# Two-part float32r weights-times-values product in the attention of a streaming encoder

## The chip, the cores and the metric

One core of one Trainium2 chip runs the whole program. The metric is device time in microseconds (us) of one execution; the kernel before takes 3136.52 us, the median of three runs (3129.24 to 3139.74).

## The reference

The reference is a two-layer encoder over 1024 positions of width 1024, all in float32. Each layer normalises, projects to 2948 columns (`w_in`), runs four mixers side by side (A: a recurrent scan, B: differential attention, C: spatial gating, D: forgetting attention, each 256 columns wide in 4 heads of 64), projects back (`w_out`), and applies a gated feed-forward with a 3-tap causal convolution. What the change concerns is the last product of B and D:

```
p1 = softmax(where(mask, s1, -1e30)); p2 = softmax(where(mask, s2, -1e30))      # B
o  = einsum('bhqk,bhkd->bhqd', p1 - lam * p2, v)                                 # [128 queries x keys] x [keys x 64]
pr = softmax(where(mask, s, -1e30)); o = einsum('bhqk,bhkd->bhqd', pr, v)        # D
```

A block of 128 queries sees the keys up to its own end, so a block has 1 to 8 groups of 128 keys.

## The kernel before, in words

The sequence is cut into two halves of 512 positions, `hf` 0 and 1. For each layer and half the program does `win` (the input projection), the mixers, `wout`, and `ffn`. The large products (`product`, `product2`, L497 and L505) take float32 weights from HBM 512 KB at a time (`wload`, L487: DMA to `wr`, ACT casts to the float32r high part, DVE subtracts to get the low part, both into `hr`), and form each 128x512 result in PSUM (`pm`, two banks) from three float32r products per 128 rows (`acc3`, L467): high x high, high x low, low x high. One 8-step product is 24 matmuls.

The mixers of one half run beside the large products of another: `body` (L1423) writes out by hand which generator is advanced when (`beside`, `weave`, `side`), and gives priorities (`PRI`). The Tile context is opened with `schedule_with_timeline_sim=True`: from these priorities and a simulated time line it fixes the order of instructions on every engine when the program is built, and the engines run their lists in that order. The half (0, 0) has its mixers beside the conditioning products `ada` of both layers and beside `win` of half (0, 1); the later ones run beside `wout`, `ffn` and `win`. `wout` of a half starts once the mixers of that half are done.

Attention, per head: `prepare` (L983) transposes the values with TensorE (`pv`), copies them (`v`, L1017) and stores them to DRAM (`vv`, tensors vB and vD: four blocks of 128 keys, two slots, 256 columns; only slot 0 is used). `values` (L1042) loads the 64 columns of one head to `V`, one DMA per half of the keys (L1053). For each of four query blocks `scores` (L1056) makes S in PSUM with float32r products, `softmax` (L1070) makes `p` with ACT, and `weighted` (L1090) does three things: TensorE transposes `p` in groups of 128 keys into a `px` bank (L1097), ACT copies up to 512 columns to SBUF (`ct`, L1106), and a float32 product per 128 keys with `ct` as the stationary operand and 64 columns of `V` moving accumulates into another `px` bank (recorded at L186, tile names px<-V,ct). ACT then scales the 128x64 result into `yB` or `yD`. At the end of every second head `out_y` (L1121) transposes y, copies it (`yst`) and stores it to `yT`, from where `wout` loads it (`yr`, split into `yh` and `yl`).

Tiles of the attention come from pool `p2` (14 pages of 128x512 float32: q, k, V, p, ct, y, yst); `prepare` uses pool `q2` (6 pages); `px` has two PSUM banks, shared by transposes and weighted products.

Of the kernel before, what the change touches and what calls it, by code (L numbers as in the profile page):

```python
# [85 lines left out]
class Kern:  # L86
    def __init__(self, tc, es, a):
# [3 lines left out]
        def pool(n, b, **k):  # L91
            return es.enter_context(tc.tile_pool(name=n, bufs=b, **k))

        PS = bass.MemoryType.PSUM
        for n, b in POOLS.items():
            setattr(self, n, pool(n, b))
# [886 lines left out]
    def prepare(self, l, hf, g, hd, finish):  # L983
# [6 lines left out]
        for t0 in (0, 2):  # L990
            ss = self.small([128, 2, ng], "qss" + g)
            xs = []
            for t in (t0, t0 + 1):
# [14 lines left out]
                for u in range(2):  # L1008
                    nc.tensor.transpose(ps[:, u * 128:u * 128 + 128], pv[:, u, :], self.ident)
                if PVR:  # L1010
                    v = self.sq([128, 2, 256], F32R, name="v")
# [30 lines left out]
    def values(self, l, hf, g, h):  # L1042
        nc = self.nc
        if PVR:
            V = []
# [44 lines left out]
    def weighted(self, p, V, scale, out):  # L1090
# [3 lines left out]
        for pc, n in p:  # L1094
            ps = self.misc()
            for j in range(0, n, 128):
                nc.tensor.transpose(ps[:, j:j + 128], pc[:, j:j + 128], self.ident)  # L1097
            if PVR:
                ch = self.s2([128, 512], F32R, name="ch")
# [9 lines left out]
        last = len(cts) - 1  # L1109
        if not PVR:  # L1110
            for b, ct in enumerate(cts):
# [239 lines left out]
NADA = 12  # L1351
MLP = True
YLP = False
PVR = False
PACE, PSTEP = 2, 2
PACING = (1, 0, 0, 0)
PA = 5000
# [18 lines left out]
P2 = True  # L1376
PRI = [(6000, 4000, 4000), (2000, 4000, 2000), (2000, 6000, 4000), (2000, 4000, 2500)]
WC = 16
POOLS = dict(cst=1, xp=8, wr=2, wp=3, hp=32, ar=4, mp=14, nt=8, nn=3, an=2, a1=9, a2=6, sm=2, p2=14, q2=6)
BANKS = dict(pm=2, pS=2, px=2, pa=1, pn=1)  # L1380


# [187 lines left out]
```

## Time and profile before

| | before |
|---|---|
| median of 3 runs | 3136.52 us |
| lowest, highest | 3129.24, 3139.74 us |
| the profiled execution: its time, its span | 3145.82 us, 3144.0 us |
| mean granted TensorE clock | 0.961 |
| PE, PEld, DVE, ACT, POOL busy | 96%, 78%, 63%, 45%, 12% |

PE is TensorE's matmuls and PEld its weight loads, which overlap them; DVE is VectorE, ACT ScalarE, POOL GpSimd, SP the engine that issues the DMAs. A line number is that of the kernel; L186, L189, L195 and L198 are helpers that record nearly every operation, so the groups there are told apart by the tiles' names. A float32 product appears as two LDWEIGHTS and two MATMUL records, a float32r product as one of each. Records print both types as f32 on PE. [...]

### The profile page before, as it was taken

How to read it: one execution, taken by the hardware profiler on the slowest of the kernel's cores; microseconds unless marked ns; L12 is line 12 of the kernel's file. 1: busy time of each engine (PE TensorE's matmuls, PEld its weight loads, DVE VectorE, ACT ScalarE, POOL GpSimd, SP SyncE). 2: the span in 40 equal slices, each digit the busy share in tenths (PEclk: the TensorE clock that was granted, in tenths of full speed). 3: DMA queues.
4: the chain of work that ended last, by engine and by line, in shares of the span. 5: the costliest groups of instructions: out<-in, count | busy, mean ns of one | idle time of the engine just before them, and what ended most of it. 6: DMA issues, size and time to landing. Idle time of an engine off the chain costs nothing. (4 is left out here: it accounts for less than half of the span.)

```text
span 3144.0 us, 48993 instructions
## 1 busy us (share of the span) xinstructions
PE 3020.1 (96%) x17440; PEld 2443.8 (78%) x17440; DVE 1980.0 (63%) x4681; ACT 1413.5 (45%) x2829; POOL 383.2 (12%) x463
## 2 busy tenths in 40 slices
PE   6999988899999999999999999999999999899999
PEld 5777767777877888777888887777888888778887
DVE  4566554567677685357777566368787675455555
ACT  3444632335454545435455443345454464333333
POOL 1010000111111011010111111020111101011111
PEclk8999977799999999999999999999999999899999
DMA  6467576443333334454343323453433232513332
GB/s 247 140 221 227 188 237 206 142 147 92 92 109 104 116 95 147 136 173 131 102 132 90 113 88 131 142 175 100 122 109 107 90 117 66 192 61 94 112 103 74
DMA packets 302195, 414.12 MB, mean 132 GB/s; under 512 B 75520, under 2 KB 174336, under 8 KB 301952
## 3 DMA queue, kind: packets, MB, share of 16 engines
q1 hardware_dynamic: 301952, 411.00, 41.7%
q8 instruction: 138, 2.26, 0.3%
q14 instruction: 105, 0.86, 0.1%
HBM read 347.66 MB, written 63.21 MB: 131 GB/s over the span
## 5 line engine op out<-in xcount | busy, mean ns | idle before, releaser
L186 PE MATMUL pm<-hh,hr 128*128 128x512 f32 (+1 forms) x4352 | 1420.9, 400 | 10.6 <-ACT hh L198 4.6
L186 PEld LDWEIGHTS pm<-hh,hr 128*128 128x128 f32 (+1 forms) x4352 | 813.4, 189 | 194.9 <-ACT hh L198 8.3
L186 PE MATMUL pm<-hl,hr 128*128 128x512 f32 x2176 | 865.4, 398 | 6.6 <-DVE hl L195 6.6
L493 ACT CAST hr<-wr 128x1024 fp32r<-128x1024 f32 (+2 forms) x496 | 427.5, 863 | 701.5 <-PE pm L186 605.0
L189 DVE TENSOR_TENSOR hr<-wr,hr 128x1024 fp32r<-128x1024 f32 (+2 forms) x496 | 511.5, 1032 | 278.3 <-ACT hr L493 254.1
L186 PEld LDWEIGHTS pm<-hl,hr 128*128 128x128 f32 x2176 | 410.7, 189 | 94.7 <-DVE hl L195 10.1
L186 PE MATMUL pm<-mh,hr 128*128 128x512 f32 x1408 | 464.6, 399 | 2.5 <-DVE y L189 1.0
L186 PEld LDWEIGHTS pm<-mh,hr 128*128 128x128 f32 x1408 | 264.0, 188 | 59.4 <-issue 1.2
L195 DVE SCALAR_TENSOR_TENSOR y<-pm,cst,y 128x511 f32<-128x511 f32 (+1 forms) x352 | 261.6, 744 | 74.1 <-ACT y L198 71.0
L195 DVE SCALAR_TENSOR_TENSOR x<-pm,cst,x 128x512 f32<-128x512 f32 x224 | 167.4, 748 | 180.2 <-PE pm L186 179.4
L186 PE MATMUL pm<-ml,hr 128*128 128x512 f32 x704 | 277.2, 394 | 0.0
L642 POOL TENSOR_TENSOR y<-y,y 128x512 f32<-128x512 f32 x88 | 117.2, 1332 | 1250.0 <-DVE y L189 423.0
L1075 DVE TENSOR_REDUCE cst<-S 128x1 f32<-128x512 f32 (+3 forms) x288 | 154.2, 551 | 97.6 <-PE S L186 96.7
L198 ACT ACTIVATE p<-S,cst 128x512 f32<-128x512 f32 (+3 forms) x288 | 165.5, 581 | 79.1 <-DVE cst L189 65.1
L186 PE MATMUL pm<-yh,hr 128*128 128x512 f32 x512 | 172.7, 413 | 6.6 <-ACT yh L600 6.6
L186 PEld LDWEIGHTS px<-V,ct 128*128 128x128 f32 x1152 | 155.3, 201 | 24.3 <-ACT ct L1106 14.2
L186 PE MATMUL px<-V,ct 128*128 128x64 f32 x1152 | 160.3, 282 | 10.6 <-ACT ct L1106 7.3
L198 ACT ACTIVATE y<-pm,cst 128x512 f32<-128x512 f32 x176 | 136.9, 778 | 67.3 <-PE pm L186 66.8
L186 PEld LDWEIGHTS pm<-ml,hr 128*128 128x128 f32 x704 | 132.7, 189 | 25.2
L647 POOL TENSOR_TENSOR ml<-th,mh 128x512 fp32r<-128x512 f32 x88 | 123.9, 1408 | 219.7 <-ACT mh L646 207.8
L189 DVE TENSOR_TENSOR cst<-cst 128x1 f32<-128x1 f32 (+6 forms) x552 | 97.5, 184 | 54.1 <-ACT p L198 46.0
L1106 ACT COPY ct<-px 128x512 f32<-128x512 f32 (+1 forms) x192 | 88.0, 479 | 95.4 <-PE px L1097 92.1
(230 smaller groups left out, 3578.7 us busy)
## 6 DMA issues: line engine op xcount, KB each, us to landing
wr<-in_up SPq DMA_DIRECT2D x176, 512.0 KB
ar<-in_ada SPq DMA_DIRECT2D x192, 256.0 KB
wr<-in_win SPq DMA_DIRECT2D x92, 512.0 KB
wr<-in_down SPq DMA_DIRECT2D x128, 256.0 KB
wr<-in_wout SPq DMA_DIRECT2D x32, 512.0 KB
ks<-qkB SPq DMA_DIRECT2D x192, 64.0 KB
wr<-in_down SPq DMA_DIRECT2D x64, 192.0 KB
k<-qkD SPq DMA_DIRECT2D x72, 128.0 KB
```

Of the source, the lines that this page charges most:

```text
L186: return self.nc.tensor.matmul(out, lhsT, rhs, start=start, stop=stop, **kw)
L189: self.nc.vector.tensor_tensor(out=out, in0=a, in1=b, op=op)
L195: self.nc.vector.scalar_tensor_tensor(out=out, in0=a, scalar=s, in1=b, op0=op0, op1=op1)
L198: self.nc.scalar.activation(out=out, in_=in_, func=func, **k)
L493: self.nc.scalar.copy(out=h, in_=r)
L642: nc.gpsimd.tensor_tensor(out=ya, in0=ya, in1=yg, op=ALU.mult)
L647: (nc.gpsimd if MLP else nc.vector).tensor_tensor(out=ml, in0=th, in1=mh.bitcast(F32), op=ALU.subtract)
L1075: nc.vector.tensor_reduce(out=nm[:, i:i + 1], in_=S_[:, 0:n], axis=AX.X, op=ALU.max, negate=True)
L1106: nc.scalar.copy(out=ct[:, 0:n], in_=ps[:, 0:n])
```

## The change

The flag `PVR` turns on and pool `p2` gets 18 pages in place of 14.

```
-PVR = False
+PVR = True
-POOLS = dict(cst=1, xp=8, wr=2, wp=3, hp=32, ar=4, mp=14, nt=8, nn=3, an=2, a1=9, a2=6, sm=2, p2=14, q2=6)
+POOLS = dict(cst=1, xp=8, wr=2, wp=3, hp=32, ar=4, mp=14, nt=8, nn=3, an=2, a1=9, a2=6, sm=2, p2=18, q2=6)
```

What the flag selects is in the code already. In `prepare`, the values are split: `v[:, 0]` is the ACT copy rounded to float32r, `v[:, 1]` is a DVE subtraction of it from PSUM (L1014), and one DMA stores both slots. In `values`, each half of the keys is loaded to a page of its own, high and low columns side by side (4 x 2 x 64 columns), by one DMA each as before. In `weighted`, the transposed weights are split as they leave PSUM, and each 128 keys take two products:

```
nc.scalar.copy(out=ch[:, 0:n], in_=ps[:, 0:n])
self.tt(cl[:, 0:n], ps[:, 0:n], ch[:, 0:n].bitcast(F32), ALU.subtract)
...
self.mm(ps[:, 0:128], ch, V[b], b == 0, False)
self.mm(ps[:, 0:64], cl, V[b][:, 0:64], False, b == last)
...
self.act(out, ps[:, 64:128], AF.Copy, scale=scale)
self.stt(out, ps[:, 0:64], scale, out, ALU.mult, ALU.add)
```

So high weights meet high and low values (128 moving columns), low weights meet high values (64 columns), and the two column halves of the result are added when it leaves PSUM.

## Rows read from the trace of the kernel before

**Rows 1.** The page's first part (busy us, share of the span, instructions) and a line of its second (tenths in 40 slices of 78.6 us).
```profile
PE 3020.1 (96%) x17440; PEld 2443.8 (78%) x17440; DVE 1980.0 (63%) x4681; ACT 1413.5 (45%) x2829; POOL 383.2 (12%) x463
PEclk8999977799999999999999999999999999899999
```

**Rows 2.** Busy time of each engine by stretches of 157.2 us: stretch, its length, then PE, PEld, DVE, ACT, POOL, each with its instructions, the granted clock, the DMA share and GB/s.
```profile
471.60:628.80 157.20, 138.85 (x1217) 112.10 (x1210) 79.64 (x245) 53.26 (x137) 13.46 (x17) 0.77 0.56 174
...
1414.80:1572.00 157.20, 154.48 (x852) 125.96 (x850) 120.77 (x309) 77.63 (x168) 20.48 (x19) 0.96 0.39 117
...
2200.80:2358.00 157.20, 155.27 (x875) 127.38 (x874) 121.43 (x276) 78.43 (x166) 25.14 (x21) 0.99 0.39 115
...
2672.40:2829.60 157.20, 140.44 (x648) 116.28 (x647) 81.63 (x153) 60.89 (x104) 17.40 (x12) 0.90 0.39 126
```

**Rows 3.** The time line of PE around three float32 products of weights and values at full clock: start us, us, what, count.
```profile
1502.83 0.78 PE L186 MATMUL px<-V,ct 128*128 128x64 f32 x6
1503.45 0.61 PE L1000 MATMUL px<-cst,pt 128*128 128x128 f32 x4
```

**Rows 4.** The same stretch on PEld, the weight loads.
```profile
1502.72 0.75 PEld L186 LDWEIGHTS px<-V,ct 128*128 128x128 f32 x6
1503.34 0.48 PEld L1000 LDWEIGHTS px<-cst,pt 128*128 128x128 f32 x4
```

**Rows 5.** The time line where three float32r products with 128 moving columns stand together (the scores of one 128-key group and the mask), ahead of large products; PE and PEld.
```profile
1169.74 0.44 PE L186 MATMUL S<-k,q 128*128 128x128 f32 x2
...
1169.96 0.19 PEld L186 LDWEIGHTS S<-hr 128*128 128x128 f32 x1
1170.02 0.27 PE L186 MATMUL S<-hr 128*128 128x128 f32 x1
1170.07 0.19 PEld L186 LDWEIGHTS pm<-mh,hr 128*128 128x128 f32 x1
1170.13 0.45 PE L186 MATMUL pm<-mh,hr 128*128 128x512 f32 x1
```

**Rows 6.** The time line of PE where one float32r product with 128 moving columns stands alone among large ones.
```profile
1110.21 0.22 PE L186 MATMUL S<-k,q 128*128 128x128 f32 x1
1110.27 0.45 PE L186 MATMUL pm<-hh,hr 128*128 128x512 f32 x1
```

**Rows 7.** Groups by shape, weight loads and matmuls: count, busy us, mean ns of one, idle time before.
```profile
L186 PEld LDWEIGHTS px<-V,ct 128*128 128x128 f32 x1152 | 155.3, 201 | 24.3 <-ACT ct L1106 14.2 <-issue 2.2 <-ACT Us L848 0.2
L186 PEld LDWEIGHTS pm<-ml,hr 128*128 128x128 f32 x704 | 132.7, 189 | 25.2
L186 PE MATMUL px<-V,ct 128*128 128x64 f32 x1152 | 160.3, 282 | 10.6 <-ACT ct L1106 7.3 <-DVE cst L189 2.8
```

**Rows 8.** Groups by shape on DVE that stand nearest to the new ones (the subtraction of a rounded copy from PSUM, narrower reads of PSUM, and the weights' low parts).
```profile
L189 DVE TENSOR_TENSOR ql<-px,qh 128x512 fp32r<-128x512 f32 x32 | 21.9, 683 | 10.8 <-ACT qh L1036 10.3 <-issue 0.2
L1075 DVE TENSOR_REDUCE cst<-S 128x1 f32<-128x384 f32 x48 | 25.8, 548 | 6.0 <-PE S L186 5.8
L1075 DVE TENSOR_REDUCE cst<-S 128x1 f32<-128x256 f32 x48 | 20.0, 417 | 9.9 <-PE S L186 9.4
L1075 DVE TENSOR_REDUCE cst<-S 128x1 f32<-128x128 f32 x48 | 13.6, 284 | 16.2 <-PE S L186 16.1
L195 DVE SCALAR_TENSOR_TENSOR U<-px,cst,U 128x128 f32<-128x128 f32 x32 | 9.1, 343 | 1.1 <-PE px L186 1.1
L189 DVE TENSOR_TENSOR D<-D,pa 128x64 f32<-128x64 f32 x16 | 3.5, 219 | 22.0 <-PE pa L186 15.6 <-ACT x L1002 6.3
L189 DVE TENSOR_TENSOR hr<-wr,hr 128x1024 fp32r<-128x1024 f32 x300 | 373.8, 1246 | 261.4 <-ACT hr L493 238.7 <-PE pm L186 5.4 <-ACT yD L198 5.3
```

**Rows 9.** Groups by shape on ACT: the copy of transposed weights, a cast of the same shape to float32r, and one of the two output scalings.
```profile
L1106 ACT COPY ct<-px 128x512 f32<-128x512 f32 x96 | 55.3, 586 | 61.2 <-PE px L1097 59.7 <-POOL acc L430 0.6
L1036 ACT CAST qh<-px 128x512 fp32r<-128x512 f32 x32 | 18.7, 585 | 28.5 <-PE px L1032 25.2 <-issue 2.9
L198 ACT ACTIVATE yD<-px,cst 128x64 f32<-128x64 f32 x64 | 20.0, 313 | 44.7 <-PE px L186 44.0
```

**Rows 10.** The time line between 2702 and 2707 us: the last head of D in half 1 of layer 1, where the granted clock is 0.50; three query blocks follow each other.
```profile
2704.07 2.66 PE L186 MATMUL px<-V,ct 128*128 128x64 f32 x12
2704.32 0.37 ACT L1106 COPY ct<-px 128x256 f32<-128x256 f32 x1 [0.50 <-PE px L1097]
2704.37 1.22 DVE L189 TENSOR_TENSOR hr<-wr,hr 128x1024 fp32r<-128x1024 f32 x1
2706.98 0.31 ACT L198 ACTIVATE yD<-px,cst 128x64 f32<-128x64 f32 x1
```

**Rows 11.** The chain that ended last, in order of time, as it passes from that head to `wout`: start us, us, what.
```profile
2723.72 0.85 PE px L186 x8
...
2724.60 0.32 ACT yD L198
...
2724.97 0.34 PE px L1125
...
2731.66 1.65 PE pm L186 x3
```

**Rows 12.** DMA: the page's line on its main queue (packets, MB, share of 16 engines' span) and the loads of V from vB.
```profile
q1 hardware_dynamic: 301952, 411.00, 41.7%
...
V<-vB SPq DMA_DIRECT2D x24, 128.0 KB
```

## The prediction, made before the change was built

> **What bounds the kernel now.** I read the page's engine shares first: PE is busy 96% of the span, DVE 63%, ACT 45% [rows 1]. The table of stretches then shows that this is no mean over unlike stages: from 1400 us on PE is near 98% wherever large products run, DVE reaches 77% at most, and the granted clock is 0.96 to 1.00. Two kinds of stretch differ: the half-0 mixers of layer 0 beside the conditioning products (clock 0.77, PE 139 of 157 us) and the end of the last mixers (clock 0.90, PE 140 of 157 us) [rows 2]. So PE's list of instructions, one behind the other, sets the end; what lies on another engine costs only where PE comes to an instruction whose input is late. The question for the change is thus threefold: does PE's own list get shorter, do waits get longer where PE has cover, and what happens at the stage ends, where it has none.
>
> **PE's list.** The number of float32 products is 576: a half has 8 heads (B and D), half 0 sees 1+2+3+4 = 10 groups of keys per head, half 1 sees 5+6+7+8 = 26, so 8 x 36 x 2 layers. Each is two weight loads and two matmuls, hence the 1152 of each [rows 7]. The change removes them and adds 576 float32r products with 128 moving columns and 576 with 64, each one load and one matmul: again 1152 and 1152. What does one cost? Six old records start at 1502.83 and the next product starts at 1503.45, 0.62 us for six [rows 3]; their loads start at 1502.72 and end their turn at 1503.34, the same 0.62 us [rows 4]. The first of the six started while its own load was already done, so five or six loads fill the time: 0.10 to 0.12 us each. Now the float32r form: three products with 128 columns start at 1169.74 and the next large one at 1170.13; the last of the three takes 0.11 us to its successor, and its load stands 0.11 us before the next load [rows 5]. A single one among large products lets the next start after 0.06 us, but that next one then takes 0.45 us where its neighbours take 0.40, so 0.11 us is paid in all [rows 6]. The load itself lasts 201 ns (float32) against 189 ns (float32r) [rows 7]. I therefore take 0.11 us a record before and after, set by the 128 columns of stationary operand, which the change does not reduce: 1152 x 0 = **0 us**. Bounds: all records at the bare 0.06 us would give 1152 x (0.06 - 0.11) = -58 us; with 0.12 us against 0.11 it is +12 us.
>
> The row says that the short product is paid by its load. [...]
>
> **DVE.** Added are 192 subtractions `cl` (96 of 512 columns, 32 each of 384, 256 and 128), priced by the same subtraction in the rows, 683 ns, and for narrower ones by reads of PSUM of that width, 548, 417 and 284 ns: 65.6 + 17.5 + 13.3 + 9.1 = 105.5 us. To these come 128 final sums of 128x64 out of PSUM, between 219 and 343 ns, nearer the first by width; at 0.25 us 32 us. And 32 subtractions of values, 417 ns, 13 us [rows 8]. Together 151 us: DVE goes from 1980 to 2131 us, 68%. In its fullest stretches it has 121 of 157 us [rows 2]; some 10 to 13 of the 192 fall in each, with their sums 10 us, so 84%. PE's large products cover this. If the cover went, all 151 us would be the price.
>
> **ACT** keeps its count: the high part takes the place of the copy, 585 against 586 ns, and the scaling of 313 ns stays [rows 9]. 0 us.
>
> **DMA and SP.** No issue is added. Each of 48 loads of V (128 KB) doubles, 6.3 MB and 24,576 packets; at the mean packet (41.7% of 16 engines' 3144 us over 301,952 packets, 69 ns) that is at most 107 us of all sixteen together, at the mean rate per MB 20 us, on engines 42% used [rows 12]. Hidden, as V is asked for ahead of the query block; the cover is thinnest at a last head. Pages: a half-1 head of D holds before q, two, k, four, V, one, y, one, p, two, ct, two: 12 of 14, and the next p the rest; afterwards 15 of 18 with one page spare behind the next p. B in half 1 goes from 14 of 14 to 17 of 18. The four pages replace what V, ch and cl take; I give them nothing.
>
> **Waits that get longer.** V's products need the output bank of `px`; with two banks it comes free only when the first group of transposed weights has left, which now needs ACT's copy and then DVE's `cl`. And the output bank is held through ACT's scaling and then DVE's sum. Per query block the chain grows by 0.28 to 0.68 us plus 0.25 us. Queued behind `cl` on DVE are the softmax maxima of the next block and the low parts of the large products' weights, 1246 ns each [rows 8].
>
> *Stage ends.* Where the last head of D closes a half, blocks follow each other with little else: at 2704 us twelve V products, a copy, a 1.22 us weight subtraction on DVE in between, and the scaling to yD [rows 10]. From the last V products the chain runs through yD and the transposes to `wout` [rows 11]. I count three such ends: this one and, by the code, those of both halves of layer 0, where `wout` waits for the mixers too. Four blocks x (0.68 + 0.25) = 3.7 us for one, 11 us for three; PE still has scores of the next block to do, so I take half, **+6 us**, bounds 0 and +11.
>
> *Elsewhere.* PE stood 7.3 us and 2.8 us before V's products for ACT's copy and a DVE operation, its loads 14.2 us [rows 7]. Now a second wait stands behind the first, on the fuller engine: I add as much again, **+10 us**. Bounds: 0, and 128 blocks x 0.93 us = +119 us if nothing covered it.
>
> **Sum:** 0 + 0 + 6 + 10 = +16 us. The profiled execution took 3145.8 us (span 3144.0), 9.3 us over the median of the three; +16 us on it is 3162 us, and against the median, which I forecast, 3152 us, 0.5% slower.
>
> **Rivals.** *Hidden (no change).* The order is planned by a simulated time line, which sees the new steps too and may place V's products later, behind large ones; PE's waits stay at some 10 us. For: waits are that small now in spite of a similar chain [rows 7]. Against: the stage ends leave little to place. 3137 to 3145 us.
>
> *The load is no limit (faster).* If float32r products of 64 or 128 columns follow each other at 0.06 us, 1152 x 0.05 = 58 us go: 3079 us; without the waits' cover 3095 us. For: the bare start distance [rows 6]. Against: the 0.11 us between loads [rows 5]. [...]
>
> *Another order that closes gaps (faster).* The whole list is planned anew, with a spare page. The stretch that ends the last mixers has 17 us without PE and about 16 us of it at half clock [rows 2]; if half of this and of the like stretch in layer 0 goes, -20 us: 3117 us. Against: nothing in the change is aimed there.
>
> *DVE crowds the large products (much slower).* Where `cl` stands ahead of a weight's low part and three weight buffers are used up, PE waits for the low part. [...] Half of the 192 `cl` at their mean of 0.55 us: +53 us, 3190 us.
>
> **Chances.** Forecast 0.43, of which a quarter ends within 0.3% (9 us, about what this measurement can tell from no change); hidden 0.24; load no limit 0.06; another order 0.13; crowding 0.14. Slower: 0.32 + 0.14 = 0.46; same: 0.11 + 0.24 = 0.35; faster: 0.19. The range leaves out the first kind of gain and the far end of crowding: 3115 to 3190 us.
>
> **What would show it.** In the changed profile: V's products on PE as 1152 records whose loads still stand 0.11 us apart (if 0.06, the first step is wrong); PE's busy time within 15 us of 3020; DVE near 2130 us with `cl` near 683 ns at full width; PE's waits before V's products around 20 us and on DVE's `cl`; the stage ends 2 us longer each. Long PE waits on the low part of weights (hr, DVE) would mean crowding; a gain with unchanged V products would mean the order.

## The result and the profile after

The changed kernel takes 3178.4 us, the median of four runs (3177.0 to 3183.1); the kernel before, run on the same chip, 3136.3 us. The ratio is 1.0148, interval 1.0121 to 1.0175: 1.5% slower. Forecast were 3152 us, range 3115 to 3190. The profiled execution took 3179.0 us (span 3177.3), 0.6 us over the median.

The page's engine shares and its clock line answer to [rows 1]:

```profile
PE 3033.6 (95%) x17440; PEld 2452.2 (77%) x17440; DVE 2111.6 (66%) x5033; ACT 1413.7 (44%) x2829; POOL 379.9 (12%) x463
PEclk8999967899999999998999999999999999899999
```

PE runs as many records as before and is busy 13.5 us longer; the span less PE's busy time went from 3144.0 - 3020.1 = 123.9 to 3177.3 - 3033.6 = 143.7 us. So of the 33.3 us between the two profiled spans, 19.8 are PE standing still and 13.5 are the same number of records lasting longer. These are two single executions, and that of the kernel before was 9.5 us over its median. DVE gained 131.6 us, ACT nothing.

The stretches of [rows 2], with the same columns, and the one in which DVE is now fullest (the second):

```profile
471.60:628.80 157.20, 140.43 (x1254) 112.74 (x1254) 91.85 (x288) 57.83 (x150) 14.97 (x20) 0.82 0.64 203
628.80:786.00 157.20, 144.62 (x755) 117.05 (x755) 130.10 (x313) 74.76 (x161) 19.62 (x17) 0.96 0.38 116
...
1414.80:1572.00 157.20, 150.85 (x814) 122.30 (x813) 120.73 (x312) 76.53 (x160) 22.44 (x21) 0.95 0.42 130
2200.80:2358.00 157.20, 148.94 (x841) 123.70 (x840) 122.62 (x298) 73.65 (x148) 22.62 (x22) 0.95 0.37 112
2672.40:2829.60 157.20, 133.79 (x663) 109.54 (x662) 83.85 (x178) 57.61 (x114) 8.35 (x5) 0.87 0.40 132
```

The two that were full (1414.8 and 2200.8) had PE at 154 to 155 of 157 us and now have it at 149 to 151. DVE's fullest stretch is at 130.1 of 157.2 us, 83%, about the 84% worked out. The stretches slide against the work, so they only hint at the place.

The groups by shape that answer to [rows 7 to 9]:

```profile
L186 PE MATMUL px<-V,ch 128*128 128x128 f32 x576 | 147.0, 308 | 7.1 <-ACT ch L1101 3.9 <-DVE cl L189 2.9 <-issue 0.3
L186 PE MATMUL px<-V,cl 128*128 128x64 f32 x576 | 138.8, 255 | 5.1 <-DVE cl L189 5.1
...
L189 DVE TENSOR_TENSOR cl<-px,ch 128x512 fp32r<-128x512 f32 x96 | 65.3, 683 | 25.3 <-ACT ch L1101 25.0
L1101 ACT CAST ch<-px 128x512 fp32r<-128x512 f32 x96 | 55.5, 585 | 72.3 <-PE px L1097 70.2 <-PE px L186 1.8
...
L195 DVE SCALAR_TENSOR_TENSOR yD<-px,cst,yD 128x64 f32<-128x64 f32 x64 | 17.8, 278 | 27.7 <-ACT yD L198 27.5
```

What was priced came out as priced: `cl` 683 ns, `ch` 585 ns, the final sum 278 ns, 1152 records for V's products. And PE's idle time just before these products is 7.1 + 5.1 = 12.2 us, against 10.6 before. The loss is real, and it does not stand where the prediction put it. The loads of the new products, on the time line of the weight loads where one block's products stand together:

```profile
1110.41 0.19 PEld L186 LDWEIGHTS px<-V,cl 128*128 128x128 f32 x1
1110.52 0.19 PEld L186 LDWEIGHTS px<-V,ch 128*128 128x128 f32 x1
1110.63 0.19 PEld L186 LDWEIGHTS px<-V,cl 128*128 128x128 f32 x1
1110.74 0.19 PEld L186 LDWEIGHTS px<-V,ch 128*128 128x128 f32 x1
```

They start 0.11 us apart, with 128 and with 64 moving columns, as in [rows 4, 5]. In the groups the new loads last as long as the float32 ones of [rows 7] did, 201 ns, and not the 189 ns of the loads taken for comparison there:

```profile
L186 PEld LDWEIGHTS px<-V,cl 128*128 128x128 f32 x576 | 116.1, 202 | 12.2 <-DVE cl L189 6.6 <-issue 1.4 <-DVE cst L189 0.2
L186 PEld LDWEIGHTS px<-V,ch 128*128 128x128 f32 x576 | 115.6, 201 | 17.8 <-ACT ch L1101 5.7 <-DVE cl L189 2.4 <-issue 2.4
```

The chain that ended last, where the last head of D hands over to `wout` [rows 11]:

```profile
2755.95 1.35 PE px L186 x7
...
2757.32 0.32 ACT yD L198
...
2757.67 0.29 DVE yD L195
...
2758.01 0.49 PE px L1125
```

From the ACT scaling to the transposes it was 0.37 us and is 0.69: the final sum adds 0.32 us at this hand-over, near the 0.25 us taken for one, and that is far from 42 us.

### The profile page after: what moved, and what is told of

The parts are those of the page before. It is cut to its first block, busy times and chain, and to the rows that moved or that the text cites. A ratio compares the mean times of both kernels' runs of the same rounds, so it can differ in the third digit from the quotient of the medians.

```text
span 3177.3 us, 49351 instructions
## 1 busy us (share of the span) xinstructions
PE 3033.6 (95%) x17440; PEld 2452.2 (77%) x17440; DVE 2111.6 (66%) x5033; ACT 1413.7 (44%) x2829; POOL 379.9 (12%) x463
## 4 chain that ended last, share of the span: by engine, by line
PE 56%; DVE 2%; DMA 2%; ACT 1%; issue 1%; SPq 1%; POOL 0%; ACTq 0%; DVEq 0%; POOLq 0%
PE pm L186 46%; PE pa L186 4%; PE px L186 2%; PE S L186 1%; PE px L1097 1%; PE pn L186 0%; DVE hr L189 0%; DMA wr<-in_wout 0%; ACT hr L493 0%; DMA yr<-yT 0%; DMA wr<-in_win 0%; PE px L1032 0%; DMA x<-xd 0%; PE px L1000 0%; PE px L1125 0%
## 5 line engine op out<-in xcount | busy, mean ns | idle before, releaser
L186 PE MATMUL px<-V,ch 128*128 128x128 f32 x576 | 147.0, 308 | 7.1 <-ACT ch L1101 3.9
L1101 ACT CAST ch<-px 128x512 fp32r<-128x512 f32 (+1 forms) x192 | 88.8, 479 | 125.2 <-PE px L1097 122.2
L186 PE MATMUL px<-V,cl 128*128 128x64 f32 x576 | 138.8, 255 | 5.1 <-DVE cl L189 5.1
L189 DVE TENSOR_TENSOR cst<-cst 128x1 f32<-128x1 f32 (+6 forms) x552 | 103.9, 193 | 45.3 <-ACT p L198 37.1
```

The lines of the kernel that those rows point to most:

```text
L186: return self.nc.tensor.matmul(out, lhsT, rhs, start=start, stop=stop, **kw)
L189: self.nc.vector.tensor_tensor(out=out, in0=a, in1=b, op=op)
L1101: nc.scalar.copy(out=ch[:, 0:n], in_=ps[:, 0:n])
```

## The experiments

Theories at the start. *Chain*: the products' wait for `cl` costs. *Load*: 151 us more on DVE crowd the large products. *Form or plan*: the float32r products, the split values, or the new page count and with it a new plan of every list. All ratios are to the kernel before on the same chip; 18 pages are meant unless told.

**e1, e3, e4, e10: parts added to the kernel before.** All four have 18 pages; e1 has nothing else.

```
e3:  + cd = self.s2([128, 512], name="cd")
     + self.tt(cd[:, 0:n], ct[:, 0:n], ct[:, 0:n], ALU.max)     # read by nothing
e10: + self.tt(cd[:, 0:n], ps[:, 0:n], ct[:, 0:n], ALU.max)     # reads the px bank too; read by nothing
e4:  as e10, and the products read cd in place of ct
```

> The kernel before with 18 pages in pool p2 and nothing else. Chain theory (the change costs because each query block waits for cl and the final sum, and the mixers of half 1 so end later, with no large products left beside them): no added step, 3136 us within 10. Order theory (any change of what the planner sees gives another order, and the order is worth tens of us): off by 15 us or more either way. If the pages alone cost, +20 to +42 us.

> The kernel before with 18 pages and 192 extra DVE operations of the size of cl, which read ct and write a page that nobody reads. Load theory (DVE's 105 us more crowd the queue): +25 to +42 us. Chain theory: nothing waits for them, 0 to +8 us. Order theory: anything within 30 us.

> The kernel before with 18 pages and a DVE operation in the place of cl, from which V's float32 products read (the maximum of the PSUM bank and its copy, so the values are the same); no float32r, no split of V, no final sum. Chain theory: cl is the larger part of the chain's growth (0.55 of 0.83 us), +22 to +32 us. Product and DMA theory (the float32r form or the doubled V costs): 0 to +5 us. Load theory: the same as for the operation beside the path.

> The kernel before with 18 pages and 192 DVE operations that read the px bank of the transposes beside its copy, as cl does, and write a page that nobody reads: the bank is held as long as with cl, but no product waits for the result. Bank theory (with two px banks the longer hold delays the next transposes or the output bank): +15 to +25 us, as with the operation in the path. Wait theory (the products' wait for DVE is what costs): 0 to +5 us.

Measured: e1 0.9995 (0.997 to 1.0019), e3 0.9989 (0.9974 to 1.0004), e10 1.0034 (1.0015 to 1.0053), e4 1.0056 (1.0036 to 1.0076). Pages, and the new plan that they bring, do nothing. As many DVE operations of nearly the same length (721 against 683 ns at full width) beside the path do nothing: load falls. The other two came out between what their theories gave. With the transposes' bank held through DVE the kernel is some 11 us slower; with the products reading the result as well it is some 17 us slower, less than the change's 42. The two intervals overlap, so in this float32 form the reading by itself, some 7 us, is not shown to cost anything.

e3 also warns how PE's waits are to be read:

```profile
PE px L186 <- ACT ct L1106: 8.8, 8, 2.0
```

Compare the changed kernel (us in total, times, longest):

```profile
PE pm L186 <- ACT p L198: 9.7, 3, 3.6
PE pm L186 <- ACT yh L600: 8.6, 4, 6.1
PE px L1097 <- ACT p L198: 8.5, 8, 2.9
PE S L186 <- DMA k<-qkD: 8.2, 4, 5.7
PE px L186 <- DVE cl L189: 8.0, 10, 2.3
...
PE pm L186 <- DVE hr L189: 1.5, 2, 1.0
```

e3 stands 8.8 us for the copy at V's products and loses nothing; the change stands 8.0 us for `cl` and loses 42. Its other waits are spread over softmax weights (`p`), keys (`k`) and y, which the change leaves as they are; the first four lines were 2.1, 6.6, 11.4 and 2.3 us in the kernel before. For the low part of the large products' weights (`hr` from DVE), the sign of crowding, PE stands 1.5 us.

**e5, e6, e7: parts taken from the changed kernel.**

```
e5:  - cl = ...; self.tt(cl, ps, ch, ALU.subtract)      # no cl; the second product reads ch
e6:  - the final self.stt(out, ps[:, 0:64], scale, out, ...)   # ACT alone scales one half
e7:  as e5, and the second product is left out
```

> The changed kernel without cl: the second product uses the high part again (the low part of the weights is left out, the high part counted twice), so the number and widths of the products, the loads of V and the final sum stay. Chain theory and load theory: 20 to 35 us under the changed kernel, so +8 to +20 us against before. Product and DMA theory: stays at +42 us.

> The changed kernel without the final sum on DVE: ACT scales columns 0 to 63 into y and the product of high weights and low values is left out of the result; cl, both float32r products and the split of V stay. Chain theory with two parts that add (cl +17 us as in the kernel before with a DVE operation in the path, the sum the rest, 25 us): +17 us. If cl alone does it in the float32r form: +42 us. If the sum is what costs: 0 to +5 us.

> The changed kernel with one float32r product per 128 keys: the low part of the weights is left out, with cl and its product; the split of V and the final sum stay. 576 weight loads and matmuls fewer on PE than before. If a short product is paid by its load (0.11 us), 576 x 0.11 = 63 us less than before: -45 to -65 us. If it is paid by its columns (0.03 to 0.06 us): -15 to -35 us.

Measured: e5 0.9988 (0.9972 to 1.0005), e6 1.0145 (1.0125 to 1.0166), e7 0.9879 (0.9859 to 0.99). In e5 the whole loss went, more than either theory gave; e6 came out as if `cl` alone were the cause; e7's gain, 1.2% or some 38 us, lies between its two theories. The float32r form, the split values, their doubled DMA and the final sum are free; everything hangs on `cl`. e7, which leaves the low part of the weights out, has 576 records fewer and beats both kernels:

```profile
PE 2950.6 (95%) x16864; PEld 2368.2 (77%) x16864; DVE 2024.5 (65%) x4841; ACT 1417.1 (46%) x2831; POOL 380.8 (12%) x463
```

and e5:

```profile
PE 3012.1 (96%) x17440; PEld 2438.4 (78%) x17440; DVE 2027.9 (65%) x4841; ACT 1411.9 (45%) x2829; POOL 381.9 (12%) x463
```

61.5 us of PE time for 576 records is 0.107 us each. The mean clock is 0.963 in both; among kernels with the same records on PE (before, e1, e3, e10) the busy time differs by up to 19 us, so the last digit is not sure. The span fell by only 3128.0 - 3094.0 = 34.0 us: 27.5 of the 61.5 came back as PE standing still.

**e2, e8, e9: the changed kernel planned or ordered otherwise.**

```
e2:  p2=18 -> p2=14
e8:  U1, U3 = 90, 80 -> 80, 70                  # the mixers' priorities
e9:  all products with ch of a block first, then all with cl
```

> The changed kernel with the 14 pages of before. Half-1 heads of B need 17 pages at once, so if the four pages only make up for V, ch and cl, the blocks can overlap less and it is slower than the changed kernel, +55 to +90 us. If pages do not matter, +42 us as the changed kernel.

> The changed kernel with the mixers advanced earlier beside the large products (U1 90 to 80, U3 80 to 70: the mixers of half 1 of both layers are handed out over fewer units). Chain theory: half 1's attention ends late, so starting it earlier gives back part of the loss: +15 to +30 us against before. Theory that the waits are spread evenly: +42 us as the changed kernel, or more since more of the attention then stands beside fewer products.

> The changed kernel with the products of a query block in another order: all high ones first, then all low ones, so that 0.1 us for each group of keys lies between ACT's copy and the first need of cl. Wait theory: part of the loss comes back, +15 to +30 us against before. Bank theory, and the theory that the steps' lengths alone count: +38 to +45 us, as the changed kernel.

Measured: e2 1.0137 (1.012 to 1.0154), e8 1.0173 (1.0146 to 1.0201), e9 1.0143 (1.0122 to 1.0164). In all three the theory that expected an effect missed, and the one that expected the loss to stay (+38 to +45 us against before, or more in e8) came out. Four fewer pages cost nothing, more urgent mixers do not buy the loss back, and giving `cl` the time of up to eight products (0.9 us) before it is wanted does not either: what hurts is not the last microsecond ahead of its first reader. That speaks against a loss that stands directly at the products, and leaves open whether `cl` hurts by being read or by being made from the `px` bank.

**e11: `cl` is made, and the second product reads `ch`.** The same instructions as in the changed kernel; the one thing that goes is that the products depend on `cl`.

```
-cts += [(ch[:, j:j + 128], cl[:, j:j + 128]) ...]
+cts += [(ch[:, j:j + 128], ch[:, j:j + 128]) ...]
```

> The changed kernel with cl computed from the px bank as it is, but the second product reads the high part again (the low part of the weights is left out of the result). Same DVE work and same hold of the bank as in the changed kernel; only the wait of the products for cl is gone. Bank theory: +35 to +42 us. Wait theory: 0 to +8 us.

Measured: 3125.7 us, 0.9978 (0.9969 to 0.9988). The whole loss is gone, and 7 us more, with DVE as full and the bank held as long (so e10's 11 us are no price of the bank that holds here). A `cl` that is not read could give its page back earlier; e2, with four pages fewer, lost no more than the changed kernel, so pages are not the reason:

```profile
PE 3009.8 (96%) x17440; PEld 2435.3 (78%) x17440; DVE 2105.5 (67%) x5033; ACT 1412.2 (45%) x2829; POOL 378.0 (12%) x463
```

This is the run that decides. Against it the changed kernel's span is 51.9 us longer: 143.7 - 115.6 = 28.1 us of PE standing still and 3033.6 - 3009.8 = 23.8 us of busy time. Of the idle time 7.7 us stand directly before V's products (12.2 against 4.5). The mean granted clock is 0.955 against 0.965. In the trace of the changed kernel it stands at one of two levels: of 6354 half microseconds 5748 have 1.00, 548 have 0.50, and 58 lie between. By these levels, as an estimate, some 286 us stand at 0.50 (2 x 0.045 x 3177.3) against 219 in e11. Two large products last 1.05 us at 0.50 and 0.62 us at 1.00 (time line below): were the 67 us more full of such products, 67 x (1 - 0.62 / 1.05) = 27 us of busy time would come from the low level, an estimate; 23.8 us were measured.

What the clock did beside pauses shows in five pauses of PE in the changed kernel's half-1 mixers of layer 0 (columns as in [rows 2]):

```profile
764.00:772.00 8.00, 4.91 (x14) 3.65 (x15) 6.07 (x17) 1.74 (x5) 0.00 (x0) 0.79 0.56 172
960.00:970.00 10.00, 4.63 (x18) 3.87 (x19) 6.36 (x18) 5.07 (x15) 0.00 (x0) 0.66 0.60 164
1062.00:1072.00 10.00, 7.08 (x24) 5.66 (x23) 7.22 (x20) 2.65 (x6) 0.00 (x0) 0.66 0.32 106
1100.00:1112.00 12.00, 8.40 (x37) 6.85 (x37) 8.65 (x21) 8.63 (x21) 2.80 (x2) 0.72 0.01 1
1163.00:1175.00 12.00, 8.99 (x32) 7.03 (x31) 9.86 (x24) 3.48 (x9) 0.50 (x1) 0.72 0.19 53
```

and in the time line of the last of them:

```profile
1163.19 0.62 PE L186 MATMUL pm<-mh,hr 128*128 128x512 f32 x2
...
1164.10 0.93 PE L1097 MATMUL px<-cst,p 128*128 128x128 f32 x7
1164.74 0.97 ACT L1101 CAST ch<-px 128x512 fp32r<-128x512 f32 x2 [0.16 <-PE px L1097]
...
1167.21 0.69 ACT L198 ACTIVATE p<-S,cst 128x512 f32<-128x512 f32 x1 [1.50 <-DVE cst L189]
...
1168.04 0.79 PE L186 MATMUL pm<-mh,hr 128*128 128x512 f32 x1 [3.01 <-ACT p L198]
...
1169.06 1.05 PE L186 MATMUL pm<-mh,hr 128*128 128x512 f32 x2
1169.08 0.68 DVE L189 TENSOR_TENSOR cl<-px,ch 128x512 fp32r<-128x512 f32 x1
...
1169.68 0.34 DVE L924 TENSOR_REDUCE cst<-T 128x16 f32<-128x192 f32 x1
...
1169.94 0.54 DVE L189 TENSOR_TENSOR cl<-px,ch 128x384 fp32r<-128x384 f32 x1
...
1174.99 0.22 PE L186 MATMUL px<-V,ch 128*128 128x128 f32 x1
```

A block's seven transposes end at 1165.03, its `ch` is there at 1165.71, and PE stands 3.01 us, by the record for the softmax of another block, whose maxima are in DVE's queue. V's products of the first block, which could run from 1165.7 on if they needed `ch` alone, come after `cl`, at 1174.99. After the pause two large products last 1.05 us (from 1169.06, at a granted clock of 0.50) in place of 0.62 (from 1163.19, at 1.00). That the pause exists because these products are planned behind `cl` is my reading of one place; what e11 shows is that with the dependence 28.1 us of idle time and 23.8 us of busy time go, over the kernel as a whole.

These five pauses belong to this one plan. In e2 and e9, which lose as much, PE's longest waits in the same half are 2.3 and 2.0 us. e9 shows the low clock there without a long wait: PE is idle for 2.6 of ten microseconds, and the clock is then 0.57 over the next ten and 0.50 from 1180 to 1190 us, though PE is busy for 9.73 and 10.00 of ten.

```profile
1150.00:1160.00 10.00, 7.41 (x31) 5.29 (x29) 9.86 (x24) 2.81 (x6) 4.01 (x4) 1.00 0.78 205
1160.00:1170.00 10.00, 9.73 (x70) 9.05 (x71) 7.70 (x33) 7.21 (x18) 0.22 (x1) 0.57 0.98 362
...
1180.00:1190.00 10.00, 10.00 (x47) 7.79 (x46) 6.84 (x25) 2.35 (x8) 0.00 (x0) 0.50 0.45 133
```

**e12: `cl` unread in one half of one layer.** Half 1 of layer 0 reads `ch` twice, all others read `cl`.

```
+self.away = (l, hf) == (0, 1)
-cts += [(ch[:, j:j + 128], cl[:, j:j + 128]) ...]
+cts += [(ch[:, j:j + 128], (ch if self.away else cl)[:, j:j + 128]) ...]
```

> As the changed kernel, but in half 1 of layer 0 alone the second product reads ch instead of cl (cl is still computed there; the low part of the weights is left out of that half's result). With cl unread everywhere 52 us of 3178 went, 39.5 us of them between the end of wout of half 0 and the start of wout of half 1 in layer 0 (760.7 to 721.2 us). Theory of the place (the wait costs where half 1 of layer 0 runs, and nearly nothing elsewhere): that stretch falls to about 721 us here too, total 3135 to 3145 us (ratio about 1.000 to 1.003). Theory of an even price (each of the 192 waits costs the same): this half has 64 of them, a third of 52 us, total about 3161 us (1.008). Theory of luck (each new plan of the lists comes out some 20 to 50 us better or worse, whichever wait is in it): no relation, the stretch stays anywhere between 720 and 760 us, and the loss may appear in another stage.

Measured: 3170.1 us, 1.0112 (1.009 to 1.0134); the named stretch takes 750.5 us. The theory of the place falls. The even price (1.008) is nearest, just outside the interval; a third of the waits bought back some 11 us, barely clear of noise, where all of them bought some 52. The stretch also lies where the theory of luck allows it, so e12 alone doesn't exclude that one; the next table speaks against it.

**All runs side by side** (ratio from all executions; span, PE's busy time and mean clock from the page of the one profiled; idle is span less busy). The profiled execution was the fastest of six in e4 (3140.3 us, median 3153.8) and e10 (3133.5, median 3144.0), and 8.3 us over the median in e12:

| products read `cl` (or DVE's copy) | ratio | span | PE busy | idle | clock |
|---|---|---|---|---|---|
| no: before | 1 | 3144.0 | 3020.1 | 123.9 | 0.961 |
| no: e1 pages | 0.9995 | 3129.7 | 3010.1 | 119.6 | 0.965 |
| no: e3 beside | 0.9989 | 3125.4 | 3000.8 | 124.6 | 0.967 |
| no: e5 high twice | 0.9988 | 3128.0 | 3012.1 | 115.9 | 0.963 |
| no: e10 bank held | 1.0034 | 3131.7 | 3007.2 | 124.5 | 0.965 |
| no: e11 unread | 0.9978 | 3125.4 | 3009.8 | 115.6 | 0.965 |
| yes, float32: e4 | 1.0056 | 3138.5 | 3019.1 | 119.4 | 0.960 |
| yes but one half: e12 | 1.0112 | 3176.6 | 3036.8 | 139.8 | 0.955 |
| yes: after | 1.0148 | 3177.3 | 3033.6 | 143.7 | 0.955 |
| yes: e2 14 pages | 1.0137 | 3173.1 | 3032.8 | 140.3 | 0.958 |
| yes: e6 no sum | 1.0145 | 3175.5 | 3044.5 | 131.0 | 0.952 |
| yes: e8 priorities | 1.0173 | 3180.6 | 3023.2 | 157.4 | 0.961 |
| yes: e9 high first | 1.0143 | 3171.7 | 3047.8 | 123.9 | 0.956 |

Each kernel is planned anew, so each is another order of the same work; yet the five that read `cl` everywhere lie between 1.0137 and 1.0173, and the six that do not between 0.9978 and 1.0034. Luck of the plan would mix them. The loss shows as idle time in one plan and as slow clock in another: e9 has no idle time more than before (123.9 us in both, the clock at 0.956 against 0.961), e8 hardly any busy time more (3023.2 against 3020.1).

By stage, cut where the last product of each `wout` with `yh` ends (profiled executions; mean of the kernels, lowest to highest; us):

| stage | six that don't read `cl` | five that do | e12 |
|---|---|---|---|
| layer 0, half 0 | 629 (621 to 640) | 631 (621 to 636) | 634 |
| layer 0, half 1 | 787 (773 to 798) | 809 (793 to 839) | 810 |
| layer 1, half 0 | 713 (707 to 721) | 717 (706 to 725) | 714 |
| layer 1, half 1 | 626 (620 to 632) | 643 (639 to 649) | 642 |

The loss lies in the two halves whose query blocks see five to eight groups of keys and thus have two `cl` each: 64 of the 96 `cl` of a layer. In layer 1 the two kinds don't overlap, and e12, which keeps the wait there, stands with those that wait. In layer 0 they overlap by 5 us, and e12, which has no wait there, did not come back: that half's share is not settled. e4, left out of the table, has 776 and 631 us in the two halves, like those that don't read `cl`.

**Open.** Why the same wait costs some 17 us with float32 products (e4), little more than the 11 of e10, and 42 with float32r ones; and in which queue a block's later products are turned into idle time or a slow clock elsewhere. That the plan, which prices each step itself, puts V's products late is argued from one place, and lateness alone does not explain the loss. From the end of ACT's copy to the start of the first product that reads it, the mean over the 576 groups of keys is 3.1 us in the kernel before, 3.9 in e11 and 4.4 in the changed kernel, but 4.2 in e10 and 4.7 in e4 (worked out from the traces' start and end times).

## Why the prediction was right, and where it was off

- **PE's list, 0 us:** right. 1152 records at 0.11 us (the loads after). That the distance goes with the 128 columns of the stationary operand agrees with loads of 64 columns in the changed kernel's trace: four take 0.36 us together (`pa<-VS,G`, 128x64, from 651.46 us), the last alone 0.14, so they start 0.07 us apart in the mean. And e5, with the new form and no `cl`, is at 0.9988. The rival that the load is no limit is excluded by the same rows and by e7's 0.107 us a record. The 189 against 201 ns, read as the two types, was no difference of type: the new float32r loads last 201 and 202 ns.
- **DVE:** the groups were right (`cl` 65.3 us at 512 columns against 65.6; the sum 278 ns against 250). The total rose by 131.6 us and not 151, since neighbouring DVE records overlap (in the time line above `cl` at 1169.08 lasts 0.68 us, and the next DVE record starts at 1169.68): e5, which has all of it but `cl`, stands 83.7 us lower, against some 105 us of `cl` durations. Its fullest stretch is at 83% as worked out. That the large products cover it: right (e3, e11). The rival of crowding, which gave 3190 us and was nearest in size, is wrong in its cause, and its sign stayed away: 1.5 us of waits for the low part of weights.
- **ACT, DMA, SP, pages, final sum, 0 us:** right (e1, e2, e5, e6).
- **Another order closes gaps:** new orders alone moved nothing (e1, e2). The "16 us at half clock" of this rival is half of the time that stood there: a mean of 0.90 from levels of 1.00 and 0.50 makes some 31 us of the 157 (2 x 0.10 x 157.2, an estimate).
- **Waits, the mis-sized step.** "Elsewhere, +10 us" was read off PE's waits just before V's products, and there they grew by 1.6 us (10.6 to 12.2). "Stage ends, +6 us" was checked at one hand-over, where the sum adds 0.32 us; the 2 us forecast for a whole end were not measured, and e6 shows that the sum adds nothing to the total. Together +16 us; measured +42. The kind was right, as e11 shows: the products' dependence on `cl` and nothing else is the loss. Its size was off in two ways. The term looked for the wait at V's products, and it turned up at other instructions: idle time rose by 19.8 us between the two profiled executions, though before V's products by 1.6. And it priced a pause at its own length, while PE also stood longer at the low clock (a mean of 0.955 against 0.961): 13.5 us more busy time (23.8 us against e11) for a list forecast at 0, of which only the records' count and their price at full clock were right. The stated upper bound, 119 us, held both. How a wait comes to stand elsewhere stays open.
- **The range** held with some luck: its upper end, 3190 us, was the price of crowding, which did not happen; the forecast's own sum is two fifths of what was measured.
- **What would show it:** PE's busy time stayed within the 15 us named, by 1.5 us, and would have been taken as a confirmation; its 13.5 us were two fifths of the loss in the profile. PE's waits before V's products, named at around 20 us, were 12.2. The rival that hid the change had these waits right (some 10 us) and the time wrong: the loss came without them.

## What to carry to other kernels

Before splitting an operand for a faster product, ask whether the product is paid by its weight load: here the loads stood 0.11 us apart with 128 and with 64 moving columns, two float32r records per 128 keys in place of two float32 ones saved nothing (e5, 0.9988), and one in place of two saved 1.2% (e7, which leaves out the low part of the weights). Price an added cross-engine step by whether the next product reads its result, not by its duration on its own engine: the same DVE work was free unread (e11) and cost 52 us read. The price does not carry over as it stands: with float32 products it was some 11 us unread (e10) and 17 us read (e4). When PE is the bound, judge a wait by idle time plus the change of PE's busy time at an equal number of records, over the whole kernel, since here the loss did not stand where the wait was made: idle time grew by 19.8 us, before V's products by 1.6.

## What was not expected of the hardware

PE's busy time went from 3009.8 us (e11, mean granted clock 0.965) to 3047.8 us (e9, 0.956) for the same 17440 records, with equal shapes and types. The low clock stood beside short pauses: around the one of 3.01 us at 1165 us the twelve microseconds had a clock of 0.72, and from 1062 to 1072 us, where PE was busy 7.08 of 10 us, it was 0.66. And it could last while PE was fully busy: from 1180 to 1190 us in e9 PE was busy for all 10 us at a clock of 0.50. Before the clock fell there, from 1150 to 1160 us, PE was busy 7.41 of 10 us.
